# TensorE, VectorE and ScalarE in a written order beside the recurrent heads of a hybrid decoder layer

## The chip, the cores and the metric

One core of one Trainium2 chip runs the whole program. The metric is device time in microseconds; a comparison of two kernels takes the median over several runs. TensorE is called PE below, VectorE DVE, ScalarE ACT, GpSimd POOL; SP (SyncE) issues most of the DMA transfers, and "SPq" in the profile is its queue.

## The reference

One decoder layer over 1024 tokens, with 16 learned meta tokens ahead of them (L = 1040), model width 1024, feed-forward width 2816, all in float32:

```python
u = rmsnorm(h, mix_norm_pre)
q, f_logit, i_in, g_out, v_pool, gate_a, gate_b = split(u @ w_in)
a = hgrn2(q, f_logit, i_in, g_out, ...)       # 4 heads of width 128, gated linear recurrence
p = multiscale_pool(v_pool, pool_proj, scale) # 4 groups, trailing windows 2, 4, 8, 16
z = sigmoid(gate_a) * (a @ w_branch_hgrn) + sigmoid(gate_b) * (p @ w_branch_pool)
h = h + rmsnorm(z @ w_out, mix_norm_post)
u = rmsnorm(h, ffn_norm_pre)
gt = causal_dwconv(u @ ffn_w_gate)
h = h + rmsnorm((gelu(gt) * (u @ ffn_w_up)) @ ffn_w_down)
# hgrn2, each head: state = f_t * state + k_t v_t ; o_t = q_t state ; o * rsqrt(mean(o*o)) * gain * sigmoid(g)
```

## The kernel before

A float32 product is made of three PE passes on split operands: a tensor is split into a rounded part (`hi`, a copy on ACT) and the rest (`lo`, a subtraction on DVE), and hi·hi, lo·hi and hi·lo are summed in a bank of PSUM. So each block of weights is loaded raw (`wraw`), cast on ACT (`whi`) and subtracted on DVE (`wlo`) before PE can use it.

The stages by the profile's time: norm and the value projection (0 to 100 us), the projections for q, f and the two gates with a Strassen scheme (100 to 326), **the heads stage** (326 to 567), the mixer's output projection (567 to 690), the two Strassen products of the feed-forward (690 to 1100), and its down projection (1100 to the end).

The change is in the heads stage. `ORDER` is a string of steps that is walked in a loop:

- `PVn`, `Gn`, `PPn`, `BBn`, `BAn`: projections of the pooled values (`ppv`), of the output gates (`pg`), inside the pool groups (`ppp`), and the two branch products (`pbb`, `pba`). A letter p, q, r, s behind the kind is one quarter of one, a and b are halves.
- `hn`: the next step of head n (`head_steps`). The 64x64 scores of a chunk are built level by level: PE multiplies k and q (`level_mm`, tile `sl`), DVE grows k, q and f for the next level (`grow`), DVE or ACT takes the scores from PSUM (`level_out`, into `near` or `sc`). The first step issues the loads of f, q, kb and k, the next one multiplies q by f on DVE and then makes the first scores on PE (tile `sb`). After the levels come transposes (`pt`), state updates (`ds`, 7 chained operations on DVE), and the outputs (`po`): ACT takes `o` from PSUM, squares it into `rs` and casts that to `rh`; DVE subtracts to get `rl` and multiplies `o` by the gate. The last step sums the squares on PE (`ms`), takes Ln and Exp on ACT (`rs`), and DVE multiplies `o` by that.
- `spn`: pooling of a group on DVE and its split; `san`: split of a head's output into `ah`, `al`.
- `wn`: kept weights. While this stage runs, feed-forward weights of the first units are loaded, summed where the Strassen scheme wants it, split (ACT `whi`, DVE `wlo`) and stored to DRAM (`kept..h`, `kept..l`): `keep_first` for n under 4, `keep_unit` behind them.

Only PE is held to the order of this walk (`tc.manual_schedule(engines={E.PE})`); what ACT and DVE do is emitted by the same walk, but a scheduler sets the order on those two. SP issues loads in its own order, and each issue waits for the buffer that it fills. `Loader` keeps weights of up to three projections ahead, each loaded and split in one go.

`put_gate`, in the stage ahead, adds up a gate tile, takes its sigmoid on ACT and stores it to DRAM (`sscr`), issued from SP; a later `load_gate` reads it back.

Of the kernel before, what the change touches and what calls it, by code (L numbers as in the profile page):

```python
# [9 lines left out]
F32R = mybir.dt.float32r  # L10
U8 = mybir.dt.uint8
AF = mybir.ActivationFunctionType
# [40 lines left out]
ZA = 4  # L53
AHEAD = 3

ORDER = ("h0 h1 PV0 PVp1 PVq1 h0 PVr1 h1 PVs1 h0 PVp2 h1 PVq2 h0 sp0 PVr2 h1 PVs2 h0 PVp3 h1 sp1 PVq3 h0 PVr3 h1 "
# [4 lines left out]
POOLED = ()  # L61
VLOAD = 8
TRUNC = False
# [6 lines left out]
def trunk_kernel(ctx: ExitStack, tc: tile.TileContext, x, meta_tokens, mix_norm_pre,  # L70
# [25 lines left out]
    def nm(s):  # L96
        cnt[0] += 1
        return f"{s}_{cnt[0]}"
# [17 lines left out]
    def wraw_tile():  # L116
        return wst.tile([P, 1024], F32, tag="wraw", name=nm("wraw"), bufs=NRAW)
# [26 lines left out]
        return t  # L144


    def wsplit(src, n_k, n_c, eng=dve):
        raw = wst.tile([P, n_k * n_c], F32, tag="wraw", name=nm("wraw"), bufs=NRAW, padded_shape=[P, 1024])
        stage["load"] = nc.sync.dma_start(raw.rearrange("p (k c) -> p k c", k=n_k), src)
        hi = wst.tile([P, n_k * n_c], F32R, tag="whi", name=nm("whi"), padded_shape=[P, 1024])  # L150
        lo = wst.tile([P, n_k * n_c], F32R, tag="wlo", name=nm("wlo"), padded_shape=[P, 1024])
        act.copy(hi, raw)
        eng.tensor_tensor(lo, raw, rr(hi), ALU.subtract)
        return [(hi.rearrange("p (k c) -> p k c", k=n_k), lo.rearrange("p (k c) -> p k c", k=n_k))]

    def wsplit2(*srcs):

        raw, (hi, lo) = wraw_tile(), (wst.tile([P, 1024], F32R, tag=t, name=nm(t)) for t in ("whi", "wlo"))
        views = [[t[:, i * 512 : (i + 1) * 512].rearrange("p (k c) -> p k c", k=4) for t in (raw, hi, lo)] for i in range(2)]
        for (r, _, _), src in zip(views, srcs):  # L160
            stage["load"] = nc.sync.dma_start(r, src)
        act.copy(hi, raw)
        dve.tensor_tensor(lo, raw, rr(hi), ALU.subtract)
        return [(h, l) for _, h, l in views]

    class Loader:

# [5 lines left out]
        def ahead(self):  # L173
            while len(self.got) < min(len(self.srcs), self.at + AHEAD):
                self.got += self.get(*self.srcs[len(self.got)])

        def next(self):
            self.at += 1
            return self.got[self.at - 1]

    def wblock(w, k0, n_k, c0, n_c):
        return w[k0 * P : (k0 + n_k) * P, c0 : c0 + n_c].rearrange("(k p) c -> p k c", p=P)
# [427 lines left out]
    def eng(op):  # L610
        return pool_e if op in POOLED else dve
# [244 lines left out]
    def put_gate(u, i, h, a, b, c=None):  # L856
        kind, j = GUNITS[u]
        m, n = 2 * j + i, ghalo(u) + HN
        at = slice(n, n + HN) if h else slice(0, n)
        g = slot(at.stop - at.start, name="sg")  # L860
        dve.tensor_tensor(g, a, b, ALU.add)
        if c is not None:
            dve.tensor_tensor(g, g, c, ALU.add)
        if kind == "F":
            put_f(m, h, g)
            return
        if kind != "Q":
            act.activation(g, g, AF.Sigmoid)
        to = dict(Q=qdr, A=sd, B=sd)[kind]
        nc.sync.dma_start(to[m + (KD if kind == "B" else 0), :, at], g)  # L870

    def load_gate(d, b, m):
        d[m] = slot(TQ, name="sa")
# [17 lines left out]
    def job(kind, i):  # L891
        if kind == "G":
            return (wblock(WIN, 0, KD, CG + i * P, P), KD, u_q, CH_Q, lambda r: post_g(i, r))
        if kind == "PV":
            return (wblock(WIN, 0, KD, CV + i * P, P), KD, u_all, CH_ALL, lambda r: post_pv(i, r))
        if kind == "PP":
            return (pool_proj[0, i].rearrange("(k c) d -> c k d", k=1), 1,
                    lambda k, lo, n: (pin[i][0][:, lo : lo + n], pin[i][1][:, lo : lo + n]), CH_Q,
                    lambda r: post_pp(i, r))
        if kind == "BA":  # L900
            return (wblock(w_branch_hgrn[0], 0, HEADS, i * P, P), HEADS, a_x, CH_Q, lambda r: post_branch(sas, i, r))
        return (wblock(w_branch_pool[0], 0, HEADS, i * P, P), HEADS, p_x, CH_Q, lambda r: post_branch(sbs, i, r))
# [36 lines left out]
    def keep_first(u):  # L939
        raw = wst.tile([P, 1024], F32R, tag="wraw", name=nm("wraw"), bufs=NRAW)  # L940
        src = rr(raw).rearrange("p (k c) -> p k c", k=KD)
        nc.sync.dma_start(src, wblock(ffn_w_gate[0], 0, KD, 2 * u * P, P))
        keep(((u, "P1"), src[:, :4]), ((u, "P2"), src[:, 4:]), lo=raw)

    def keep_unit(u, w):
        ab = []
        for h in range(2):
            t = wraw_tile().rearrange("p (k c) -> p k c", k=4)
            nc.sync.dma_start(t, wblock(w, 4 * h, 4, 0, 2 * P))
            ab.append(t)  # L950
        a11, a21, a12, a22 = ab[0][:, :, :P], ab[0][:, :, P:], ab[1][:, :, :P], ab[1][:, :, P:]
        if u >= EARLY:
            keep(((u, "P1"), a11), ((u, "P2"), a12))
            yield
        ADD, SUB = ALU.add, ALU.subtract
        keep(((u, "P6"), ((a21, ADD, a22), (None, SUB, a11))), ((u, "P5"), ((a21, ADD, a22),)))
        yield
        keep(((u, "P3"), ((a21, ADD, a22), (None, SUB, a11), (a12, SUB, None))), ((u, "P7"), ((a11, SUB, a21),)))
        yield
        keep(((u, "P4"), a22))  # L960
        yield

    keeps = [keep_unit(0, ffn_w_gate[0]), keep_unit(UP0, ffn_w_up[0])]

    order = ORDER.split()
    order = [(o_[:-1], int(o_[-1])) for o_ in order]
# [59 lines left out]
    with tc.manual_schedule(engines={E.Activation, E.DVE, E.PE}):  # L1026
# [79 lines left out]
        for e in range(0, EARLY, 2):  # L1106
            p = gates.start_pair(e)
            for f in [f[i] for i in range(2) for f in p]:
                f()
                for j in SUMS_AT.get(13, ()) if e == 0 else ():  # L1110
# [5 lines left out]
    jobs_ = [(k.rstrip("ap"), i) for k, i in order if k[0].isupper() and k[-1] not in "bqrs"]  # L1116
    branch = [o_ for o_ in jobs_ if o_[0] in ("BA", "BB")]
    assert jobs_[-len(branch) :] == branch
    loader = Loader([job(*o_)[:2] + (P, eng("w%s%d" % o_)) for o_ in jobs_[: -len(branch)]]
                    + [tuple(job(*o_)[0] for o_ in branch[i - i % 2 : i - i % 2 + 2]) for i in range(len(branch))],  # L1120
                    lambda *a: wsplit(*a) if len(a) == 4 else wsplit2(*a))

    def split_z(c, k):
        n = len(TILES[c]) * P
# [11 lines left out]

    z0 = []
    gens, after, halves_of = {}, {}, {}
    with tc.manual_schedule(engines={E.PE}):
        for kind, i in order:  # L1140
            if kind == "sp":
                pool_split(i)
                continue
            if kind == "w":
                keep_first(i) if i < EARLY else next(keeps[i - EARLY])
                continue
            if kind == "sa":
                ahl[i] = split(heads[i]["o"], "a")
                continue
            if kind == "h":  # L1150
                if i not in gens:
                    gens[i] = head_steps(i)
                next(gens[i], None)
                continue
            kind, part = kind.rstrip("abpqrs"), kind[-1]
            src, n_k, xs, chunks, post = job(kind, i)
            if part in "qr":
                next(halves_of[kind, i])
                continue
            if part in "bs":  # L1160
                banks = next(halves_of[kind, i])
                loader.ahead()
                pay()
                after[kind, i] = post(banks)
                continue
            if kind in ("BA", "BB"):
                load_gate(sas if kind == "BA" else sbs, kind == "BB", i)
            ws = loader.next()
            if (kind, i) == ("BA", KD - 1):
                z0 = [split_z(0, k) for k in range(ZA)]  # L1170
            if part in "ap":
                halves_of[kind, i] = proj_parts(None, 0, n_k, xs, chunks, ws=ws, name="p" + kind.lower(),
                                                cuts=(n_k // 2,) if part == "a" else range(n_k // 4, n_k, n_k // 4))
                next(halves_of[kind, i])
                continue
            banks = proj(None, 0, n_k, xs, chunks, ws=ws, name="p" + kind.lower(),
                         by_bank=2 if (kind, i) == ("BA", KD - 1) else 0)
            loader.ahead()
            pay()
            after[kind, i] = post(banks)  # L1180
            if kind == "BA":
                dve.tensor_tensor(sas[i], sas[i], sbs[i], ALU.add)
                z[i] = sas[i]
# [622 lines left out]
```

## Time and profile before

| | us |
|---|---|
| median of 3 runs (lowest, highest) | 1319.91 (1318.8, 1320.88) |
| profiled execution, its own time | 1317.88 |
| span of the profiled execution | 1316.2 |
| PE busy | 1290.6 (98%) |
| DVE busy | 961.2 (73%) |
| ACT busy | 522.5 (40%) |
| POOL busy | 359.9 (27%) |

The time around the span is 1.7 us. PE is the engine with next to no idle time, so what another engine does costs only where PE waits for it. Durations of DVE and ACT instructions in the profile are those of one; queued behind each other they start about 0.09 us sooner than these add up to.

### The profile page before, as it was taken

To read this page: it belongs to the slowest core of one execution; us is meant where nothing else is said; L and a number is where in the kernel's file an instruction comes from. 1 tells how busy PE (TensorE), PEld (TensorE's weight loads), DVE (VectorE), ACT (ScalarE), POOL (GpSimd) and SP (SyncE) were. 2 spreads that over 40 slices of the span, in tenths; PEclk is the share of its full clock that TensorE was granted. 3 is DMA by queue.
4 is the path that set the end of the run, shared out by engine and by line. 5 is a ranking of instruction groups with operands and counts; after the bars stand their busy time and mean duration, and the time that the engine had idled before them with its cause. 6 is when DMAs were issued, how large, how long until landed. Compare 5 with 4: busy or idle time off the path is not lost.

```text
span 1316.2 us, 21988 instructions
## 1 busy us (share of the span) xinstructions
PE 1290.6 (98%) x8650; PEld 1139.7 (87%) x8650; DVE 961.2 (73%) x1293; ACT 522.5 (40%) x904; POOL 359.9 (27%) x307
## 2 busy tenths in 40 slices
PE   8999999999999899999999999999999999999998
PEld 7799899998998788978898888888888888888887
DVE  6768965454685887675588999888988985455758
ACT  5554533333134737226564222222332223444443
POOL 3015333230000000160035555554755652000000
PEclk9999999999999899999999999999999999999999
DMA  8135543334524566876677776667677699666644
GB/s 275 42 106 173 197 156 103 107 105 138 174 71 147 193 225 215 291 235 250 237 256 248 193 211 185 172 196 192 167 180 172 131 267 300 208 224 224 225 174 161
DMA packets 143802, 247.62 MB, mean 188 GB/s; under 512 B 11000, under 2 KB 75164, under 8 KB 143698
## 3 DMA queue, kind: packets, MB, share of 16 engines
q1 hardware_dynamic: 131634, 221.83, 49.6%
q0 software_dynamic: 12064, 24.38, 11.0%
q8 instruction: 68, 1.11, 0.3%
q14 instruction: 36, 0.29, 0.1%
HBM read 174.11 MB, written 95.09 MB: 205 GB/s over the span
## 4 chain that ended last, share of the span: by engine, by line
PE 91%; DVE 3%; DMA 2%; ACT 2%; issue 1%; SPq 0%; DVEq 0%; ACTq 0%
PE P L306 17%; PE P L307 17%; PE P L309 17%; PE pd L186 5%; PE pd L188 5%; PE pd L187 5%; PE pm L186 2%; PE pm L188 2%; PE pm L187 2%; PE ppv L206 1%; PE ppv L210 1%; PE pg L206 1%; PE ppv L207 1%; PE pv L187 1%; PE pv L186 1%
## 5 line engine op out<-in xcount | busy, mean ns | idle before, releaser
L307 PE MATMUL P<-v,whi 128*128 128x512 f32 (+2 forms) x408 | 140.7, 353 | 0.0
L306 PE MATMUL P<-v,whi 128*128 128x512 f32 (+2 forms) x408 | 140.7, 352 | 0.0
L309 PE MATMUL P<-v,wlo 128*128 128x512 f32 (+2 forms) x424 | 135.1, 349 | 0.0
L277 POOL TENSOR_TENSOR swa<-wraw,wraw 128x512 f32<-128x512 f32 x32 | 51.1, 1598 | 186.1 <-DMA wraw<-in_w_in_dram 79.8
L251 ACT CAST whi<-wraw 128x512 fp32r<-128x512 f32 x90 | 53.1, 618 | 102.4 <-PE P L307 75.9
L1516 DVE TENSOR_TENSOR rot<-wraw,rot 128x1024 fp32r<-128x1024 f32 x31 | 38.0, 1224 | 72.3 <-ACT rot L1515 72.3
L306 PEld LDWEIGHTS P<-v,whi 128*128 128x128 f32 x408 | 76.7, 188 | 10.4
L307 PEld LDWEIGHTS P<-v,whi 128*128 128x128 f32 x408 | 76.6, 188 | 10.2
L309 PEld LDWEIGHTS P<-v,wlo 128*128 128x128 f32 x424 | 74.0, 188 | 10.8
L187 PE MATMUL pd<-rot 128*128 128x512 f32 x274 | 82.5, 388 | 0.0
L188 PE MATMUL pd<-rot 128*128 128x512 f32 x274 | 82.5, 388 | 0.0
L186 PE MATMUL pd<-rot 128*128 128x512 f32 x274 | 81.9, 388 | 0.1
L252 DVE TENSOR_TENSOR wlo<-wraw,whi 128x512 fp32r<-128x512 f32 x86 | 76.4, 911 | 2.7 <-ACT whi L251 2.7
L251 ACT CAST whi<-swa 128x512 fp32r<-128x512 f32 x64 | 38.1, 619 | 92.6 <-PE P L307 77.8
L252 DVE TENSOR_TENSOR wlo<-swb,whi 128x512 fp32r<-128x512 f32 x64 | 66.4, 1045 | 10.4 <-ACT whi L251 10.4
L1515 ACT CAST rot<-wraw 128x1024 fp32r<-128x1024 f32 x31 | 32.7, 1054 | 90.8 <-PE pd L188 89.4
L306 PE MATMUL P<-uhi,whi 128*128 128x258 f32 (+2 forms) x240 | 68.5, 303 | 0.0
L307 PE MATMUL P<-ulo,whi 128*128 128x258 f32 (+2 forms) x240 | 68.4, 303 | 0.0
L251 ACT CAST whi<-swb 128x512 fp32r<-128x512 f32 x64 | 38.1, 618 | 71.6 <-PE P L307 67.1
L306 PE MATMUL P<-t4h,whi 128*128 128x258 f32 (+2 forms) x228 | 65.5, 304 | 0.0
L307 PE MATMUL P<-t4l,whi 128*128 128x258 f32 (+2 forms) x228 | 65.4, 304 | 0.0
L306 PE MATMUL P<-t2h,whi 128*128 128x258 f32 (+2 forms) x228 | 65.3, 304 | 0.0
(386 smaller groups left out, 3840.1 us busy)
## 6 DMA issues: line engine op xcount, KB each, us to landing
wraw<-in_w_in_dram SPq DMA_DIRECT2D x36, 512.0 KB, 4.2
yt<-ysum SPq DMA_DIRECT2D x33, 512.0 KB, 5.1
wraw<-in_ffn_w_gate_dram SPq DMA_DIRECT2D x26, 512.0 KB, 6.0
wraw<-in_ffn_w_up_dram SPq DMA_DIRECT2D x22, 512.0 KB, 6.0
wsum<-in_ffn_w_down_dram SPq DMA_DIRECT2D x22, 512.0 KB, 8.5
wraw<-in_w_out_dram SPq DMA_DIRECT2D x18, 512.0 KB, 4.4
ysum<-ys SPq DMA_DIRECT2D x11, 768.0 KB, 5.2
sa<-sscr SPq DMA_DIRECT2D x16, 513.0 KB, 5.3
```

Of the source, the lines that this page charges most:

```text
L186: pe.matmul(ps, ahi, bhi, start=first, stop=False)
L187: pe.matmul(ps, ahi, blo, start=False, stop=False)
L188: pe.matmul(ps, alo, bhi, start=False, stop=last)
L206: pe.matmul(ps[:, :n], whi[:, k, :], xhi, start=(k == 0), stop=False)
L251: act.copy(hi, src)
L252: (pool_e if 4 <= i < 2 * self.early else dve).tensor_tensor(lo, src, rr(hi), ALU.subtract)
L277: pool_e.tensor_tensor(s1, a21, a22, ALU.add)
L306: pe.matmul(d, whi[:, k, :], xh[:, c : c + w], start=(k == 0 and onto is None), stop=False, **go)
L307: pe.matmul(d, whi[:, k, :], xl[:, c : c + w], start=False, stop=False, **go)
L309: pe.matmul(x[:, o : o + w], wlo[:, k, :], xh[:, c : c + w], start=False, stop=(k == 3), **go)
L1515: act.copy(hi, src)
L1516: dve.tensor_tensor(lo, src, rr(hi), ALU.subtract)
```

## The change

It makes these edits:

- ACT and DVE join PE in the written order inside the heads stage: each takes its instructions in the order in which the walk emits them, and an instruction that waits holds up all that stands behind it on its engine.
- `ORDER` is written anew: heads 0 and 1 step every quarter from the start, heads 2 and 3 run on into the `BB` projections, the `BB` projections come as halves throughout, and the `w` steps are smaller and more.
- `Loader` becomes `Loader2`: the raw load is issued apart from the split, one projection further ahead; splits stay two ahead.
- `keep_first` and `keep_unit` yield between the load and the split.
- The sigmoid gates' stores are issued from ACT; the stores of `qdr` stay on SP.

```diff
-ORDER = ("h0 h1 PV0 PVp1 PVq1 h0 PVr1 h1 PVs1 h0 PVp2 h1 PVq2 h0 sp0 PVr2 h1 PVs2 h0 PVp3 h1 sp1 PVq3 h0 PVr3 h1 "
-         "PVs3 h0 sp2 Gp2 h1 Gq2 h0 h2 Gr2 h1 Gs2 h0 sp3 Gp3 h1 h2 Gq3 h0 h3 Gr3 h1 h2 Gs3 h0 PP0 h2 PP1 h1 h3 PP2 "
...
+ORDER = ("h0 h1 PVp0 PVq0 h0 PVr0 h1 PVs0 h0 PVp1 h1 PVq1 h0 PVr1 h1 PVs1 h0 sp0 PVp2 h1 PVq2 h0 sp1 PVr2 h1 PVs2 "
+         "h0 PVp3 h1 PVq3 h0 sp2 PVr3 h1 PVs3 h0 Gp2 h1 Gq2 h0 h2 sp3 Gr2 h1 Gs2 h0 h2 Gp3 h1 h3 Gq3 h0 h2 Gr3 h1 "
+         "h3 Gs3 h2 sa0 PP0 h3 PP1 h2 PP2 h3 sa1 PP3 h2 BBa0 h3 BBb0 h2 w0 BBa1 h3 BBb1 h2 w0 w1 BBa2 h3 BBb2 h2 w1 "
+         "w4 BBa3 h3 h2 w4 BBb3 h3 BBa4 h2 BBb4 h3 w4 BBa5 h2 BBb5 h3 w4 w5 BBa6 sa2 BBb6 h3 w5 BBa7 w5 BBb7 sa3 "
+         "BA0 w5 BA1 w5 w2 BA2 w2 w3 BA3 w3 BA4 BA5 BA6 BA7")
...
+    class Loader2:
+        def __init__(self, srcs):
+            self.srcs, self.raws, self.got, self.at, self.split = srcs, [], [], 0, 0
+            self.load()
+            self.load()
+            self.ahead()
...
+        def ahead(self):
+            while self.split < len(self.srcs) and len(self.got) < self.at + 2:
+                src, raw = self.srcs[self.split], self.raws[self.split]
+                self.got += wsplit2(raw) if len(src) == 2 else wsplit(*src[:3], raw=raw)
+                self.split += 1
+            if len(self.raws) <= self.split:
+                self.load()
...
-        if kind != "Q":
-            act.activation(g, g, AF.Sigmoid)
-        to = dict(Q=qdr, A=sd, B=sd)[kind]
-        nc.sync.dma_start(to[m + (KD if kind == "B" else 0), :, at], g)
+        if kind == "Q":
+            nc.sync.dma_start(qdr[m, :, at], g)
+            return
+        act.activation(g, g, AF.Sigmoid)
+        act.dma_start(sd[m + (KD if kind == "B" else 0), :, at], g)
...
         nc.sync.dma_start(src, wblock(ffn_w_gate[0], 0, KD, 2 * u * P, P))
+        yield
         keep(((u, "P1"), src[:, :4]), ((u, "P2"), src[:, 4:]), lo=raw)
+        yield
...
-    keeps = [keep_unit(0, ffn_w_gate[0]), keep_unit(UP0, ffn_w_up[0])]
+    keeps = [keep_first(u) for u in range(EARLY)] + [keep_unit(0, ffn_w_gate[0]), keep_unit(UP0, ffn_w_up[0])]
...
-    with tc.manual_schedule(engines={E.PE}):
+    with tc.manual_schedule(engines={E.PE, E.Activation, E.DVE}):
...
-                keep_first(i) if i < EARLY else next(keeps[i - EARLY])
+                next(keeps[i])
```

Line numbers in and behind the head steps grow by some 30 (L794, the gate product of `o`, becomes L825, L714 becomes L745, L802 becomes L833).

Two places are shown. The first is DVE around the outputs of head 0. In the kernel before, where `q_3400`, `k_3398` and `f_3397` are head 0, `..3408` head 1, `..4289` head 2, `..4500` head 3, and `o_4608` is head 0's output, it reads:

```order
L711 COPY_PREDICATED near_4417<-mask_145,sl_4543 128x64x2
L673 TENSOR_TENSOR k_4498<-k_4498,f_4497 128x528
L681 TENSOR_TENSOR f_4286<-f_4286 128x264
L771 SCALAR_TENSOR_TENSOR st_4523<-st_4523,f_3405,ds_4527 128x128
L153 TENSOR_TENSOR wlo_4601<-wraw_4598,whi_4600 128x128
L771 SCALAR_TENSOR_TENSOR st_4523<-st_4523,f_3405,ds_4536 128x128 x3
L153 TENSOR_TENSOR wlo_4656<-wraw_4653,whi_4655 128x128
L794 SCALAR_TENSOR_TENSOR o_4608<-o_4608,par,sg_4610 128x1026
L673 TENSOR_TENSOR k_4287<-k_4287,f_4286 128x132x4
L679 TENSOR_TENSOR q_4289<-q_4289,f_4286 128x128x4
L711 COPY_PREDICATED near_4417<-mask_152,sl_4666 128x32x4
```

Head 2 and head 3 were begun before head 0's output came: its product `o_4608` stands among level steps of head 2 and the state updates of head 1. In the changed kernel, where `o_4429` and `rl_4458` are head 0's, `q_4352` is head 2 and `o_4528`, `rl_4557` are head 1's, DVE reads:

```order
L157 TENSOR_TENSOR wlo_4420<-wraw_4247,whi_4419 128x128
L864 TENSOR_TENSOR rl_4458<-rs_4430,rh_4457 128x1026
L825 SCALAR_TENSOR_TENSOR o_4429<-o_4429,par,sg_4431 128x1026
L745 TENSOR_TENSOR q_4352<-q_4352,f_4349 128x512
L704 TENSOR_TENSOR k_4350<-k_4350,f_4349 128x528
L708 TENSOR_TENSOR q_4352<-q_4352,f_4349 128x1024
L712 TENSOR_TENSOR f_4349<-f_4349 128x528
L752 COPY_PREDICATED near_4465<-mbase,sb_4470 128x256
```

Now the first multiplication of head 2's q stands behind `rl` and the product of head 0. PE in the changed kernel has, at the same place, the outputs of head 0 (`po`), the first scores of head 2 (`sb`), and then the gate projection (`pg`):

```order
L820 MATMUL po_4446<-q_3396,st_4329 128x128
L819 MATMUL po_4446<-sc_3450,vh_3823 128x128
L820 MATMUL po_4446<-q_3396,st_4329 128x128
L750 MATMUL sb_4470<-q_4352,kb_4351 32x32 x32
L237 MATMUL pg_4507<-uhi_88,whi_4243 128x342
L238 MATMUL pg_4507<-ulo_89,whi_4243 128x342
```

No projection stands between `po` and `sb` there. The second place is DVE around the last step of heads 0 and 1. In the kernel before, head 3's first multiplication, of `q_4500`, stands among the state updates `st` of heads 0 and 1, with both outputs still to come:

```order
L681 TENSOR_TENSOR f_4286<-f_4286 128x528
L771 SCALAR_TENSOR_TENSOR st_4477<-st_4477,f_3397,ds_4481 128x128 x4
L771 SCALAR_TENSOR_TENSOR st_4477<-st_4477,f_3397,ds_4490 128x128 x3
L714 TENSOR_TENSOR q_4500<-q_4500,f_4497 128x512
L771 SCALAR_TENSOR_TENSOR st_4523<-st_4523,f_3405,ds_4527 128x128 x2
```

In the changed kernel the first multiplication of head 3 (`q_4564`) stands behind head 1's last product, `o_4528` by `rs_4529`:

```order
L712 TENSOR_TENSOR f_4349<-f_4349 128x264
L742 COPY_PREDICATED near_4465<-mask_145,sl_4601 128x64x2
L833 TENSOR_TENSOR o_4528<-o_4528,rs_4529 128x1026
L745 TENSOR_TENSOR q_4564<-q_4564,f_4561 128x512
L704 TENSOR_TENSOR k_4562<-k_4562,f_4561 128x528
L708 TENSOR_TENSOR q_4564<-q_4564,f_4561 128x1024
```

And PE there has the sums of squares of head 1 (`ms`), and directly behind them the first scores of head 3:

```order
L830 MATMUL ms_4660<-rl_4557,onesr 128x342
L829 MATMUL ms_4664<-rh_4556,onesr 128x342
L830 MATMUL ms_4664<-rl_4557,onesr 128x342
L750 MATMUL sb_4678<-q_4564,kb_4563 32x32 x32
L237 MATMUL pg_4507<-uhi_88,whi_4243 128x342
```

Head 3's scores moved from ahead of the outputs of heads 0 and 1 on DVE to behind the last operation of head 1.

More of the change, by code (lines that the diff above doesn't have):

```diff
@@ L144, in gain_bc, with wload, wsplit @@
         return t
-    def wsplit(src, n_k, n_c, eng=dve):
+    def wload(src, n_k, n_c):
         raw = wst.tile([P, n_k * n_c], F32, tag="wraw", name=nm("wraw"), bufs=NRAW, padded_shape=[P, 1024])
         stage["load"] = nc.sync.dma_start(raw.rearrange("p (k c) -> p k c", k=n_k), src)
+        return raw
+    def wsplit(src, n_k, n_c, eng=dve, raw=None):
+        raw = wload(src, n_k, n_c) if raw is None else raw
         hi = wst.tile([P, n_k * n_c], F32R, tag="whi", name=nm("whi"), padded_shape=[P, 1024])
@@ L154, in wsplit, with wload2, wsplit2 @@
         return [(hi.rearrange("p (k c) -> p k c", k=n_k), lo.rearrange("p (k c) -> p k c", k=n_k))]
[L156 to L161, printed above, removed]
+    def wload2(*srcs):
+        raw = wraw_tile()
+        for i, src in enumerate(srcs):
+            stage["load"] = nc.sync.dma_start(raw[:, i * 512 : (i + 1) * 512].rearrange("p (k c) -> p k c", k=4), src)
+        return raw
+    def wsplit2(raw):
+        hi, lo = (wst.tile([P, 1024], F32R, tag=t, name=nm(t)) for t in ("whi", "wlo"))
         act.copy(hi, raw)
         dve.tensor_tensor(lo, raw, rr(hi), ALU.subtract)
-        return [(h, l) for _, h, l in views]
+        return [tuple(t[:, i * 512 : (i + 1) * 512].rearrange("p (k c) -> p k c", k=4) for t in (hi, lo)) for i in range(2)]
     class Loader:
@@ L175, in ahead, with next, load @@
                 self.got += self.get(*self.srcs[len(self.got)])
+        def next(self):
+            self.at += 1
+            return self.got[self.at - 1]
+    class Loader2:
[4 more added lines that the diff above has]
+            self.ahead()
+        def load(self):
+            if len(self.raws) < len(self.srcs):
+                src = self.srcs[len(self.raws)]
+                self.raws.append(wload2(*src) if len(src) == 2 else wload(*src[:3]))
+        def ahead(self):
[5 more added lines that the diff above has]
+                self.load()
         def next(self):
@@ L950, in keep_unit @@
             ab.append(t)
+        yield
         a11, a21, a12, a22 = ab[0][:, :, :P], ab[0][:, :, P:], ab[1][:, :, :P], ab[1][:, :, P:]
@@ L1118, in trunk_kernel @@
     assert jobs_[-len(branch) :] == branch
-    loader = Loader([job(*o_)[:2] + (P, eng("w%s%d" % o_)) for o_ in jobs_[: -len(branch)]]
-                    + [tuple(job(*o_)[0] for o_ in branch[i - i % 2 : i - i % 2 + 2]) for i in range(len(branch))],
-                    lambda *a: wsplit(*a) if len(a) == 4 else wsplit2(*a))
+    loader = Loader2([job(*o_)[:2] + (P,) for o_ in jobs_[: -len(branch)]]
+                     + [tuple(job(*o_)[0] for o_ in branch[i - i % 2 : i - i % 2 + 2]) for i in range(0, len(branch), 2)])
     def split_z(c, k):
```

3 rows, old and new, of the table ORDER are left out of this document.

## The prediction

> **What bounds the kernel now.** I read the page first, its busy times and its chain of what ended last:
>
> ```profile
> span 1316.2 us, 21988 instructions
> PE 1290.6 (98%) x8650; PEld 1139.7 (87%) x8650; DVE 961.2 (73%) x1293; ACT 522.5 (40%) x904; POOL 359.9 (27%) x307
> PE 91%; DVE 3%; DMA 2%; ACT 2%; issue 1%; SPq 0%; DVEq 0%; ACTq 0%
> ```
>
> PE is idle for 25.6 us in all. The change takes no work from PE, so it can win only where PE waits or runs at a lower clock, and can lose wherever a new wait reaches PE. The next view is the table of busy times by stretch (us, then PE, PEld, DVE, ACT, POOL busy, the granted clock, DMA share, GB/s):
>
> ```profile
> 100.00:326.00 226.00, 225.32 (x1498) 207.98 (x1496) 144.73 (x193) 86.13 (x152) 71.06 (x49) 1.00 0.42 139
> 326.00:567.00 241.00, 227.34 (x2782) 216.57 (x2783) 173.44 (x291) 98.64 (x179) 11.44 (x22) 0.98 0.58 192
> ```
>
> The heads stage holds 241.00 − 227.34 = 13.66 us of idle PE; the gates stage ahead of it holds 0.68. DVE is busy 72% of the heads stage and ACT 41%, so neither is full; what matters is in which order they serve PE. The list of PE's waits between 320 and 567 us (total, times, longest) names the releasers:
>
> ```profile
> PE ms L798 <- DVE phis L842: 2.6, 1, 2.6
> PE po L788 <- DVE near L711: 2.0, 1, 2.0
> PE sl L696 <- ACT rs L800: 1.8, 1, 1.8
> PE sl L690 <- DVE q L679: 1.6, 1, 1.6
> PE sl L696 <- DVE near L711: 1.5, 1, 1.5
> PE pba L206 <- DVE sa L879: 1.2, 1, 1.2
> PE ms L799 <- DVE rl L833: 1.2, 1, 1.2
> ```
>
> All come from DVE or ACT; no row there names a weight (`whi`, `wlo`). The same table in finer stretches shows what a wait does to the clock:
>
> ```profile
> 425.90:426.70 0.80, 0.76 (x3) 0.79 (x4) 0.80 (x3) 0.80 (x3) 0.00 (x0) 0.50 0.50 200
> 426.70:429.20 2.50, 2.50 (x15) 2.50 (x14) 2.50 (x5) 0.03 (x1) 0.00 (x0) 0.53 0.02 7
> 441.00:443.00 2.00, 2.00 (x52) 1.96 (x45) 2.00 (x5) 1.97 (x3) 0.00 (x0) 0.50 0.70 264
> 443.00:446.00 3.00, 3.00 (x13) 3.00 (x12) 2.42 (x4) 2.73 (x4) 0.00 (x0) 0.50 0.31 110
> 450.00:470.00 20.00, 16.68 (x320) 15.18 (x319) 20.00 (x38) 10.79 (x18) 0.00 (x0) 1.00 0.65 212
> ```
>
> Behind the wait of 2.0 us (it ends at 425.9) PE runs at 0.50 to 0.53 for 3.3 us, which loses 0.8 × 0.5 + 2.5 × 0.47 = 1.6 us. Behind the two waits of 2.6 and 1.8 us the clock is 0.50 from 441 to 446, a loss of 2.5 us. Between 450 and 470, with 3.3 us idle in shorter pieces, it stays at 1.00. So the stage pays 13.7 + 1.6 + 2.5 = **17.8 us** for its waits. That is the ceiling of what the change can win here.
>
> **The change part by part.** First the edits that I cost at nothing. The gate stores leave SP for ACT:
>
> ```profile
> 324.60 0.32 SPq L870 DMA_DIRECT2D sscr<-sg  x1
> SPq L870 <- ACT sg L868: 43.1, 14, 6.7
> SPq L149 <- DVE wlo L153: 44.5, 6, 13.6
> ```
>
> One issue takes 0.32 us of SP; 32 of them are 10 us of ACT, in a stage of 226 us in which ACT has 140 us free. Even at twice the price (20 us) the cover holds, so nothing, between −0.7 (the stage's whole idle time) and +1. SP no longer stands behind sigmoids (43.1 us of waiting in the stretch from 250 us on), so loads behind these stores leave earlier; but no PE wait names a load. The same holds for the raw loads one projection ahead: SP waits 44.5 us there for a free buffer, and PE for none of those weights. Gain nothing; if the cover were gone it would show as PE waits for `wlo`.
>
> Now the written order. An instruction on DVE or ACT that waits now holds all that stands behind it. I walked the new order by hand from 326.2 us, with the durations of these rows:
>
> ```profile
> L833 DVE TENSOR_TENSOR rl<-rs,rh 128x1026 fp32r<-128x1026 f32 x4 | 4.9, 1218 | 0.0
> L794 DVE SCALAR_TENSOR_TENSOR o<-o,par,sg 128x1026 f32<-128x1026 f32 x4 | 5.1, 1285 | 1.8 <-ACT phis L841 1.3 <-ACT rs L792 0.5
> L802 DVE TENSOR_TENSOR o<-o,rs 128x1026 f32<-128x1026 f32 x4 | 4.9, 1225 | 2.4 <-ACT rs L801 2.4
> L714 DVE TENSOR_TENSOR q<-q,f 128x512 f32<-128x512 f32 x4 | 2.8, 688 | 6.0 <-DMA q<-qscr 6.0
> L819 DVE TENSOR_TENSOR_SCAN s<-vp 128x1040 f32<-128x1040 f32 x3 | 6.9, 2309 | 0.0
> L801 ACT ACTIVATE rs<-rs 128x1026 f32<-128x1026 f32 x4 | 4.2, 1062 | 0.0
> ```
>
> *First place, outputs of head 0.* PE goes from `po` of head 0 straight to `sb` of head 2, which needs `q`; on DVE that stands behind head 0's `rl` and `o`. ACT's timeline shows the chain ahead of `rl` in the kernel before, for head 1:
>
> ```profile
> 431.26 0.59 ACT L791 COPY o<-po 128x512 f32<-128x512 f32 x1 [1.20 <-PE po L789]
> 431.88 1.06 ACT L792 ACTIVATE rs<-o 128x1026 f32<-128x1026 f32 x1
> 432.97 1.06 ACT L832 CAST rh<-rs 128x1026 fp32r<-128x1026 f32 x1
> ```
>
> From the last `po` the copy, the square and the cast take 432.97 + 1.06 − 431.26 = 2.8 us, then DVE 1.22 + 1.29 + 0.69 = 3.2: 6.0 us, less 0.2 for overlapped starts, in which PE has nothing: **5.8 us** (6.4 if nothing overlaps and each hand-over costs 0.1).
>
> *Second place, last step of head 1.* PE goes from `ms` straight to `sb` of head 3. Its `q` stands on DVE behind head 1's last product, and that waits for Ln, a table load and Exp on ACT:
>
> ```profile
> 439.95 1.42 ACT L800 ACTIVATE rs<-ms,eps_t 128x342 f32<-128x342 f32 x3
> 441.39 1.28 ACT L801 ACT_TABLE_LOAD   x1
> ```
>
> The last of three Ln (1.42 / 3 = 0.5), the load 1.28, Exp 1.06, then DVE 1.23 + 0.69: 4.8 us from the last `ms`. If the first table load (the Ln side, as long) isn't done ahead, all three Ln come late: 4.8 + 0.9 + 1.28, 7.0. I take **5.3**, nearer to the lower end, since the first load waits for no data. [...]
>
> Both places leave PE idle for longer than any wait of before, so the clock must fall behind each: 1.6 to 2.5 us each by the rows above, 2.1 taken, **4.2** for both. [...]
>
> *Start of the stage.* The order has `sb` of head 1 after three quarters only. DVE's timeline of before:
>
> ```profile
> 335.04 0.71 DVE L673 TENSOR_TENSOR k<-k,f 128x528 f32<-128x528 f32 x1 [2.85 <-DMA k<-kscr]
> 337.70 0.69 DVE L714 TENSOR_TENSOR q<-q,f 128x512 f32<-128x512 f32 x1 [1.94 <-DMA q<-qscr]
> ```
>
> These DVE waits are for DMA; PE stood on other projections. In the new order PE reaches `sb` of head 1 at about 335.5, an estimate of three quarters and a first `sb` behind 326.2; `q` of head 1 lies on DVE behind head 0's k and three more operations. With the loads 1.6 us earlier (no sigmoid ahead of them on SP), it is ready at 337 to 338: **2.0 us**, between 0 and 3.5, and clock 0.8 (0 to 1.6).
>
> *Around 380 us.* The level steps of head 0 stand on DVE behind a `wlo` (1.23) that waits for ACT, and a pooling scan (2.31): 3.5 us of foreign work less what a PE quarter covers. **2.0**, 0 to 3.5.
>
> *PP projections, and the rest up to the BB ones.* The nearest rows are the waits at L798 and L696 (2.6 and 1.8) in the same part. **2.0**, 0 to 4.
>
> *Kept weights.* `w` steps put `wlo` and `whi` of feed-forward weights on DVE and ACT between the additions that free PE's banks (`sa`, L879). They wait for loads that SP issues behind stores of other kept weights:
>
> ```profile
> SPq L937 <- ACT whi L922: 35.6, 12, 5.1
> L920 DVE TENSOR_TENSOR wlo<-wraw,wraw 128x512 f32<-128x512 f32 x6 | 4.0, 687 | 6.1 <-DMA wraw<-in_ffn_w_gate_dram 3.6 <-DMA kept7l<-wlo 2.5
> ```
>
> Before, DVE could do another addition meanwhile; PE waited 1.2 us for L879. Now a late load delays all of them. At worst two of SP's longest waits or so (5.1 + 3.6, about 8); at best nothing, since loads are issued a step ahead. **3.0.**
>
> Sum of what is new: 5.8 + 5.3 + 4.2 + 2.0 + 0.8 + 2.0 + 2.0 + 3.0 = 25.1 us. I count all of the 17.8 as gone, since each of those waits came of where the scheduler had put a DVE or ACT operation. The balance is +7.3: 1317.88 + 7.3 = 1325.2 for a profiled execution, whose own time lies 2.0 under the median of the runs shown, so **1327** against the median.
>
> **The rivals.** *Faster: PE waits at the two places only.* If loads are early enough and every other new wait is covered by the projection beside it, and the clock doesn't fall, the new cost is 5.8 + 5.3 = 11.1 against 17.8: 1319.9 − 6.7 = 1313. For it speaks that DVE has 28% of the stage free and that heads 0 and 1 start earlier; against it the clock rows, and the DMA waits on DVE at the start. *No change.* The two places with their clock (15.3) and 2.0 in the PP part, nothing else: 17.3 against 17.8, 1319. *Kept weights decide.* If SP's stores delay the loads by its longest waits, that term is 8 and the clock falls again (2.5), 7.5 more than forecast: 1335; it decides once the loads land over 3 us behind the addition that follows. For it speaks a DMA share of 0.58 over the stage, against it the loads issued a step ahead. That the change might do less than it says is only possible for the stores and loads, which I count at nothing anyway.
>
> **How the numbers follow.** Forecast 1327: 0.48. Faster rival 1313: 0.30. No change 1319: 0.10. Kept weights 1335: 0.12. A change of 0.2% (2.6 us) is about what the measurement tells from none: faster 0.30, same 0.10, slower 0.60. The range: below the forecast it takes in the faster rival with one of its two places 4 us shorter, 1309; above, the start, 380, PP and table-load terms at their upper ends with the kept weights at theirs would give 1327 + 2.3 + 1.5 + 2 + 1.7 + 7.5 = 1342, and as they won't all meet I end at 1338. The forecast's own case spans 1321 to 1333.
>
> **What would show it.** Right: PE idle for 5 to 6 us between the `po` of head 0 and the next `sb`, released by DVE `q`, with a granted clock near 0.5 behind it; the same behind `ms` of head 1; the waits at L711 and L842 gone. ACT in the gates stage longer busy, PE there unchanged. Wrong: PE idle in the stage under 10 us in all, or `q` of heads 2 and 3 done before these places; or waits of PE for `whi`, `wlo`, which I count at nothing.

## The result, and the profile after

The changed kernel is slower: 1.0279 of the time before (95% interval 1.0242 to 1.0316), 1352 to 1361 us against 1320.4 in the same comparison. One execution of it at 2143 us and a clock of 0.556 is left out of the ratio. The profiled execution took 1352.1 us, 34.2 more than that of before. The direction was as forecast, the size was not: 7 us were forecast.

The page of the changed kernel, its busy times and its chain that ended last:

```profile
span 1350.4 us, 21954 instructions
PE 1299.5 (96%) x8650; PEld 1147.6 (85%) x8650; DVE 969.1 (72%) x1293; ACT 524.4 (39%) x905; POOL 353.3 (26%) x307
PE 64%; DVE 3%; ACT 3%; issue 1%; DMA 1%; DVEq 0%; SPq 0%; ACTq 0%
```

PE's idle time went from 25.6 to 50.9 us, and the same 8650 matmul records now take 8.9 us longer: 25.3 + 8.9 is the whole difference. Nearly all of both lies in the heads stage, which now ends at about 601 us (table of busy times by stretch):

```profile
335.00:343.00 8.00, 7.92 (x159) 7.59 (x160) 4.77 (x7) 0.00 (x0) 0.34 (x4) 0.80 0.59 228
420.00:430.00 10.00, 9.96 (x122) 9.71 (x123) 2.84 (x4) 1.36 (x4) 0.00 (x0) 0.82 0.01 2
440.00:450.00 10.00, 5.70 (x147) 5.43 (x147) 5.63 (x9) 4.72 (x7) 0.00 (x0) 0.66 0.09 26
500.00:510.00 10.00, 3.62 (x13) 3.62 (x14) 4.63 (x8) 2.34 (x5) 0.00 (x0) 0.50 0.51 196
326.00:601.00 275.00, 235.64 (x2792) 224.37 (x2792) 177.42 (x293) 101.06 (x181) 9.02 (x21) 0.93 0.48 162
100.00:326.00 226.00, 225.62 (x1499) 208.09 (x1498) 145.76 (x193) 85.88 (x152) 70.10 (x49) 1.00 0.43 138
```

275.00 − 235.64 is 39.4 us idle, against 13.7 before, at a mean clock of 0.93. The gates stage ahead, with the stores now on ACT, is as it was. PE's waits in the changed kernel (total, times, longest):

```profile
PE sb L750 <- issue: 12.6, 2, 6.6
PE pbb L237 <- ACT kt L783: 10.4, 1, 10.4
PE po L819 <- ACT rs L831: 3.0, 1, 3.0
PE sl L721 <- DVE q L710: 2.8, 1, 2.8
PE pm L217 <- DVE sa L911: 2.3, 1, 2.3
PE sb L750 <- DMA kb<-kbscr: 2.3, 1, 2.3
...
PE pba L238 <- DVE al L864: 1.8, 1, 1.8
...
PE pba L237 <- ACT ah L863: 1.1, 1, 1.1
```

The two `sb` waits are the two places of the forecast. "issue" means that the view names no releaser; the timelines of ACT and then DVE do. At the first place:

```profile
414.12 0.59 ACT L822 COPY o<-po 128x512 f32<-128x512 f32 x1 [1.20 <-PE po L820]
414.74 1.06 ACT L823 ACTIVATE rs<-o 128x1026 f32<-128x1026 f32 x1
415.83 1.05 ACT L863 CAST rh<-rs 128x1026 fp32r<-128x1026 f32 x1
```

```profile
416.91 1.23 DVE L864 TENSOR_TENSOR rl<-rs,rh 128x1026 fp32r<-128x1026 f32 x1 [6.01 <-ACT rh L863]
418.05 1.28 DVE L825 SCALAR_TENSOR_TENSOR o<-o,par,sg 128x1026 f32<-128x1026 f32 x1
419.25 0.69 DVE L745 TENSOR_TENSOR q<-q,f 128x512 f32<-128x512 f32 x1
```

DVE stands idle for 6.0 us, with head 2's `q` ready to be done (its load was issued at 393.99, and the slowest of the four such loads landed after 6.4 us), because head 0's `rl` is first in line; PE starts `sb` at 420.04, 5.96 us after its last `po`.

The 10.4 us lie at 496 to 506. The chain of waits there, in order of time:

```profile
488.54 9.24 DMA kept1l<-wraw
497.86 3.87 DMA wraw<-in_ffn_w_gate_dram
501.76 0.70 DVE wlo L952
...
505.84 0.49 ACT kt L783
506.38 0.65 PE pbb L237
```

And SP's own wait:

```profile
SPq L983 <- DMA kept1l<-wraw: 7.9, 1, 7.9
```

A store of kept weights holds one of the three raw buffers; the second load of the next unit (`w4`) can be issued only when that store has landed, 9.2 us after its issue. DVE waits 8.1 us in line with the sum `wlo` for that load, ACT 13.1 us in line with the cast behind it, and behind them stand the operations that free PE's banks: `sa` on DVE and `kt` on ACT. PE, out of banks, waits its 10.4 us for `kt`.

### The profile page after: what moved, and what is told of

It is laid out like the page before. It is cut to its first block, busy times and chain, and to the rows that moved or that the text cites. A ratio compares the mean times of both kernels' runs of the same rounds, so it can differ in the third digit from the quotient of the medians.

```text
span 1350.4 us, 21954 instructions
## 1 busy us (share of the span) xinstructions
PE 1299.5 (96%) x8650; PEld 1147.6 (85%) x8650; DVE 969.1 (72%) x1293; ACT 524.4 (39%) x905; POOL 353.3 (26%) x307
## 4 chain that ended last, share of the span: by engine, by line
PE 64%; DVE 3%; ACT 3%; issue 1%; DMA 1%; DVEq 0%; SPq 0%; ACTq 0%
PE P L338 11%; PE P L337 11%; PE P L340 11%; PE pd L217 5%; PE pd L219 5%; PE pd L218 5%; PE pm L217 2%; PE pm L219 2%; PE pm L218 2%; PE pba L238 1%; PE pba L237 1%; PE pba L241 1%; PE pbb L237 1%; PE pbb L241 1%; DMA kept1l<-wraw 1%
## 5 line engine op out<-in xcount | busy, mean ns | idle before, releaser
L337 PEld LDWEIGHTS P<-v,whi 128*128 128x128 f32 x408 | 76.7, 188 | 10.4
```

The source lines that it names most:

```text
L337: pe.matmul(d, whi[:, k, :], xh[:, c : c + w], start=(k == 0 and onto is None), stop=False, **go)
```

## The experiments

**DVE and ACT to the scheduler, all else as changed.**

```diff
-    with tc.manual_schedule(engines={E.PE, E.Activation, E.DVE}):
+    with tc.manual_schedule(engines={E.PE}):
```

> The changed kernel, but DVE and ACT are left to the scheduler again in the heads stage; the new ORDER, the loads ahead, the kept weights in pieces and the stores from ACT stay. Theory A (the written order on DVE and ACT makes the stalls, since an instruction that waits holds all behind it): the waits of 6.0 us before sb of head 2 and 6.6 us before sb of head 3 and the wait of 10.4 us at pbb shrink to below 3 us each, and the time falls from about 1356 to 1315-1328 us. Theory B (the new ORDER, the loads or the stores are what costs, whoever orders DVE): the waits stay and the time stays above 1345 us.

Measured: 1314.8 us, ratio to before 0.9961 (0.9948 to 0.9974). Theory A holds: the written order on these two engines costs 3.2% (1.0279 / 0.9961 = 1.032), about 42 us, and what is left of the change wins 0.4%. PE's largest waits there:

```profile
PE sb L750 <- DMA kb<-kbscr: 2.8, 2, 1.6
PE sb L750 <- ACT rs L831: 2.0, 1, 2.0
PE ms L830 <- DVE rl L864: 1.5, 1, 1.5
```

**One engine at a time.** `engines={E.PE, E.Activation}`:

> The changed kernel with ACT and PE in the written order and DVE left to the scheduler. Theory A says that the cost is DVE's line (q of heads 2 and 3 behind products of heads 0 and 1): most of the 42 us between the changed kernel (1356) and the version with both left to the scheduler (1315) goes, 1317 to 1332 us. If ACT's line is what costs (its casts of kept weights ahead of evictions), it stays above 1340.

`engines={E.PE, E.DVE}`:

> The changed kernel with DVE and PE in the written order and ACT left to the scheduler. Theory A: the waits before sb of heads 2 and 3 (6.0 and 6.6 us) stay nearly whole, since DVE still waits in line for Square, Ln and Exp, and so does the wait behind the kept weights' load: 1340 to 1358 us. If ACT's line is what costs: below 1332.

Measured: 1328.6 us with ACT in line (1.0060, 1.0045 to 1.0076), 1339.6 with DVE in line (1.0138, 1.0112 to 1.0163). Against both free (0.9961) that is 1.0% and 1.8%, some 13 and 23 us of the 42. With DVE alone in line the `sb` waits are whole, the one behind the load at `pbb` is gone, and a new one stands behind the sums of the kept weights, for head 3's `al`:

```profile
PE sb L750 <- issue: 12.6, 2, 6.6
PE pba L238 <- DVE al L864: 5.8, 1, 5.8
```

With ACT alone in line 2.0 us are left of the `sb` waits, as with both engines free, and of the 10.4 us 3.6 are left, at a later `po`, since `kt` still stands on ACT behind a cast that waits for a sum of the kept weights:

```profile
PE po L819 <- ACT kt L783: 3.6, 1, 3.6
```

The two `sb` waits are DVE's line. The 10.4 us come only with both in line; each line alone has a smaller wait behind the kept weights. The two parts add up to 36 of the 42 us, and both hold a longer wait at the mixer's start (`pm`, 5.8 us with DVE in line and 4.2 with ACT, against 0.7). The lists name DVE's `sa` as what released PE there. DVE's part lay a little under the expected stretch, since I had expected that wait to stay too.

**Heads 2 and 3 moved ahead.**

```diff
-Gs2 h0 h2 Gp3 ... Gr3 h1 h3 Gs3
+Gs2 h2 h0 Gp3 ... Gr3 h3 h1 Gs3
```

> The changed kernel with head 2's step moved ahead of head 0's outputs, and head 3's ahead of head 1's last step, in ORDER; all else as changed. Theory A says that the two waits of 6.0 and 6.6 us and the lower clock behind them (about 3.5 us more) go: 14 to 16 us less than the changed kernel, about 1341 us. Rival: the chain from po over ACT to DVE only meets the next PE instruction that needs DVE, and less than 6 us are won, above 1350 us.

Measured: 1350.4 us (1.0235, 1.0208 to 1.0261), about 6 us won, the rival's side of the forecast, though hardly clear of the noise (the interval overlaps that of the changed kernel). DVE's timeline shows why the second place is only half mended, 4.6 us in place of 6.6:

```profile
434.19 1.23 DVE L833 TENSOR_TENSOR o<-o,rs 128x1026 f32<-128x1026 f32 x1 [2.68 <-ACT rs L832]
...
437.46 0.71 DVE L745 TENSOR_TENSOR q<-q,f 128x512 f32<-128x512 f32 x1
```

Head 3's `q` now stands behind head 0's last product, which waits for Exp as head 1's did. And PE's wait at the mixer's start (`pm`) grew from 2.3 to 7.3 us. There the timelines of DVE and POOL show splits of z that take 0.41 us elsewhere:

```profile
589.33 2.64 DVE L1163 TENSOR_TENSOR zc<-sa,zc 128x256 fp32r<-128x256 f32 x1
...
592.37 5.38 DVE L1163 TENSOR_TENSOR zc<-sa,zc 128x256 fp32r<-128x256 f32 x1
```

```profile
588.28 3.40 POOL L1258 TENSOR_TENSOR wlo<-wraw,whi 128x1024 fp32r<-128x1024 f32 x1 [153.29 <-ACT whi L1256]
...
592.78 4.67 POOL L1258 TENSOR_TENSOR wlo<-wraw,whi 128x1024 fp32r<-128x1024 f32 x2
```

**The same, with that subtraction on DVE.**

```diff
-            pool_e.tensor_tensor(lo, raw, rr(hi), ALU.subtract)
+            dve.tensor_tensor(lo, raw, rr(hi), ALU.subtract)
```

> The version with heads 2 and 3 moved ahead, and the low part of the first output weights (w_out) subtracted on DVE in place of GpSimd. In the version without this, DVE's small splits of z took 2.64 and 5.38 us in place of 0.41 while GpSimd subtracted, and PE waited 7.3 us for them. If the two engines stand in each other's way there: the splits take 0.41 us, PE's wait at pm falls below 3 us, and the time is 1343 to 1347 us against 1350.4. If the splits are long for another reason: the wait stays and the time is 1350 or more.

Measured: 1344.0 us (1.0180, 1.0164 to 1.0197), 6.4 less; no split of z is over 0.56 us, and `pm` waits 2.4:

```profile
L1163 DVE TENSOR_TENSOR zc<-sa,zc x24: 417/549/561, 588.1 to 674.0; 128x384 fp32r<-128x384 f32 x16, 128x256 fp32r<-128x256 f32 x8
PE pm L217 <- DVE sa L911: 2.4, 1, 2.4
```

By these runs about half of what the move of the heads had won was lost at the end of the stage, where DVE met GpSimd; the eight subtractions of output weights on DVE, 1.22 us in each of the three that its timeline up to 600 us shows, cost less. Both edits together win 12 us, near theory A's 14 to 16. The changed kernel with the second edit alone was not run, so how much of the 6.4 us would come there too stays open.

**One sum of the kept weights later.**

```diff
-BBa3 h3 h2 w4 BBb3 h3 BBa4 h2 BBb4 h3 w4 BBa5
+BBa3 h3 h2 BBb3 h3 BBa4 h2 BBb4 h3 w4 w4 BBa5
```

> The changed kernel with one step of the kept weights, the split of the first unit's sums that waited for its load (w4, second step), moved 2 projections later, beside the next w4 step. Theory C (the 10.4 us wait is DVE and ACT standing in line behind a load that SP could issue only when a store of another kept weight had freed the buffer): the wait of 10.4 us goes, and 8 to 13 us are won with its clock, about 1346 us. Rival: the load is later still by its neighbours on the DMA queues and the wait only moves to the new place: over 1352 us.

Measured: 1347.7 us (1.0210, 1.0180 to 1.0241), 9 less, within theory C's stretch. The 10.4 us are gone, but another wait grew from 3.0 to 7.7:

```profile
PE po L819 <- ACT rs L831: 7.7, 1, 7.7
```

Here Ln of head 2 stands on ACT behind casts of the kept weights, and these behind the sums on DVE. So the load was the cause of the long wait, and the sums themselves, in line, are the next one.

**All named places mended, all three engines in line.**

```diff
-Gs2 h0 h2 Gp3 h1 h3 Gq3 h0 h2 Gr3 h1 h3 Gs3 h2 sa0 PP0 h3 PP1 h2 PP2 h3 sa1 PP3
+h2 Gs2 h0 Gp3 h1 h3 Gq3 h2 Gr3 h3 h0 h1 Gs3 h2 PP0 h3 PP1 sa0 h2 PP2 h3 PP3 sa1
...
(w4 from its second step on, and w5, w2 and w3, some projections later)
```

> All three engines in the written order as in the changed kernel, with the named places mended in ORDER: head 2's first scores a projection quarter ahead of head 0's outputs, head 3's ahead of the last steps of both heads 0 and 1, the splits of heads 0 and 1 two projections later, and the sums of the kept weights behind the last of the heads' steps. If the named waits are the cause (theories A and C), of the 12.6 us before sb some 10 go, of the 10.4 and 3.0 us behind the kept weights some 12, and of the lower clock some 5: 1326 to 1334 us. Rival: a written order only hands a wait on to the next instruction that needs DVE, as in the two runs that mended one place each (6 and 9 us won): 1338 to 1348 us.

Measured: 1347.5 us (1.0211, 1.0195 to 1.0226): the rival. One of the `sb` waits is still 4.2 us, and most of the others are new ones; all PE waits of the stage add up to 32.4 us, against 39.8 in the changed kernel. The longest:

```profile
PE sb L750 <- DVE q L745: 5.8, 2, 4.2
PE pbb L237 <- ACT rs L831: 5.8, 1, 5.8
PE pba L237 <- ACT whi L168: 3.9, 2, 3.4
PE sb L750 <- DMA kb<-kbscr: 3.9, 2, 2.5
PE pba L237 <- DVE sa L911: 3.6, 3, 2.0
PE ppp L237 <- ACT sg L655: 3.0, 1, 3.0
```

That two lines cannot be written well by hand is not shown by this; it is shown that none of these four versions, mended at their longest waits, comes near the scheduler.

**The small edits.** The gate stores from ACT, alone on the kernel before (the `put_gate` part of the diff):

> The kernel before, with nothing but the gate stores issued from ACT. All theories: within 0.2% of before, 1317 to 1323 us, since no wait of PE names a load in the heads stage. If the 32 issues on ACT delay the weights' casts in the gates stage, PE would wait for whi there and the time would rise by over 3 us.

Measured: 1319.5 us, ratio 1.0003 (0.9992 to 1.0014). Nothing, as forecast. `Loader2` alone on the kernel before:

> The kernel before with the changed kernel's loader alone (raw loads a projection ahead, splits two ahead). If the 4.9 us by which the loader tells the two versions with the new ORDER apart is its own: 1313 to 1317 us. If it is worth nothing by itself, as forecast, and only meets the new ORDER well: 1318 to 1322 us.

Measured: 1319.5, ratio 0.9995 (0.9984 to 1.0005). Nothing either. The loader of before with the new ORDER, DVE and ACT to the scheduler:

> DVE and ACT left to the scheduler, the new ORDER, but the loader of the kernel before (load and split in one go, three projections ahead). If the raw loads one projection ahead are worth nothing, as forecast: 1313.5 to 1316.5 us, as the version with the new loader (1314.8). If the 4.4 us won over the kernel before come of the loader: back at 1318 to 1320.

Measured: 0.9994 (0.9979 to 1.0008). So the new ORDER alone wins nothing and the new loader alone wins nothing; only together do they win the 0.4%. In the profile the mixer's start (`pm`) waits 3.6 us with the old loader and 0.7 with the new one. Why the two need each other stays open, the more so as the runs with the old loader spread over 9 us.

**Versions beyond.** Heads 2 and 3 ahead, DVE and ACT to the scheduler:

> The new ORDER with head 2's step ahead of head 0's outputs and head 3's ahead of head 1's last step, DVE and ACT left to the scheduler. If PE's remaining wait of 2.0 us before sb of head 3 there goes with nothing in its place: 1311 to 1314 us, against 1314.8 without the move. Rival: the scheduler places head 3's q early anyway and its po waits instead: 1314 to 1317.

Measured: 1315.8 us, 0.9963 (0.9949 to 0.9978): the same as without it. The wait before `sb` is now 3.0 us, not gone. Heads 0 and 1 a quarter later:

```diff
-PVp0 PVq0 h0 PVr0 h1 PVs0 h0 PVp1 ... h1 h3 Gs3 h2
+PVp0 PVq0 PVr0 h0 PVs0 h1 PVp1 h0 ... h0 h3 Gs3 h1 h2
```

> The new ORDER with DVE and ACT left to the scheduler, and all steps of heads 0 and 1 one projection quarter later, up to the PP projections. In the version without the shift PE waits 2.8 us for kb at the first scores and 2.0 us before sb of head 3. If both go: 1309.5 to 1312 us. If the heads' end comes later by the quarter and is missed at the end of the BB projections: 1314 to 1318 us.

Measured: 1314.2 us, 0.9956 (0.9941 to 0.9971). Both leading `sb` waits shrink (1.6 us in all), `ppp` waits longer; it is the fastest one here and beats both kernels, though not clearly the version with nothing shifted.

## Why the prediction was wrong

**What held.** That written lines on DVE and ACT turn their waits into PE's was right at the two places and at 380 us, where a `wlo` that waits for ACT and then a scan stand on DVE ahead of a head's level steps, as forecast. Term by term, in us of idle PE: first place 5.8 forecast, 6.0 measured; second 5.3, 6.6; at 380 us 2.0, 2.8; PP projections and the rest 2.0, 2.6 (four waits of 0.4 to 1.0, for which no instruction had been named). The stores were worth nothing, as the row of the gates stage and the run with them alone show. The waits of before are gone, as forecast, but for 0.9 us at the first `ppv`.

The start agrees by luck, 2.0 and 2.3. The forecast had head 1's scores late, behind three quarters; they came without a wait. PE waited before the scores of head 0, which `ORDER` puts behind two quarters, for a load:

```profile
335.04 1.08 PE L750 MATMUL sb<-q,kb 128*32 128x32 f32 x64 [2.26 <-DMA kb<-kbscr]
```

The kernel before has no such wait, and with DVE and ACT left to the scheduler it stays (2.8 us, in the list of that run): it comes of the new `ORDER`, not of the written lines.

On ACT the second place reads:

```profile
437.25 1.28 ACT L831 ACT_TABLE_LOAD   x1
438.55 1.42 ACT L831 ACTIVATE rs<-ms,eps_t 128x342 f32<-128x342 f32 x3
439.98 1.28 ACT L832 ACT_TABLE_LOAD   x1
441.27 1.06 ACT L832 ACTIVATE rs<-rs 128x1026 f32<-128x1026 f32 x1
```

That is the chain of the forecast, and longer than its 5.3 because ACT came to head 1's Ln only after head 0's Ln and Exp, each with a table load of its own, so that the load for its Ln was not done ahead. The forecast had this case, at 7.0, and took a value near its lower end. Each load took 1.28 us, and the one of the Exp began 0.01 us behind the Ln. That a load can stand done ahead of its data the kernel before shows: there one ran from 499.58 to 500.86 us, and its Ln, waiting for `ms`, began at 502.29.

**What failed: the term for the kept weights.** It was 3.0, with 8 at most. Measured: 10.4 + 3.0 + 1.1 + 1.8 = 16.3 us, in all of which PE stood behind kept-weight work in the two lines: for `kt` and `sa`, for head 2's Ln, and for head 3's `ah` and `al`. ACT's timeline at the second of these waits:

```profile
529.88 0.62 ACT L954 CAST whi<-wlo 128x512 fp32r<-128x512 f32 x1 [1.36 <-DVE wlo L952]
530.51 1.28 ACT L831 ACT_TABLE_LOAD   x1
```

The mechanism was named, with its end (banks freed late; for `ah` and `al` it was operands that came late); what I mis-sized was the load. I took it as issued a step ahead and priced its delay by SP's longest waits of before (5.1 + 3.6). In the kernel before such a wait is covered, since the scheduler gives DVE something else; so its rows hold no such price. The new one is 9.2 us for the store, then 3.9 for the load, then the sums, one behind the other. It was priced as one late load; PE waited in four places.

**And the clock.** The forecast had 5.0 us for it (4.2 and 0.8), in place of 4.1 that went. PE's busy time grew by 8.9, so the clock took about 13 in all, an estimate that takes the 4.1 as gone: after the 10.4 us it stood at 0.50 for the rest of 500 to 510, and after the start it cost 1.6 (8 us at 0.80) where 0.8 was taken. Behind the 3.0 us and behind the 1.1 and 1.8 it was 0.83 (530 to 540 and 550 to 560). So most of the missed waits cost twice, but not each of them: behind the 2.8 us at 384 us the clock stayed at 1.00.

**What was not in it.** 2.3 us at the mixer's start, for which no term stood. A DVE split of z that takes 0.15 us elsewhere took 2.37 there, while GpSimd subtracted (from 596.86 us, for 2.71):

```profile
597.22 2.37 DVE L1167 TENSOR_TENSOR zc<-sa,zc 128x2 fp32r<-128x2 f32 x1
```

No run takes this out of the changed kernel by itself, so its price there is read from the trace alone.

Sum: 38.9 us of idle PE are in these terms, against 20.1 forecast. With the 0.9 us at `ppv` it is 39.8; 0.4 of that lie behind 601 us, and the rest are the stage's 39.4. The kept-weights case was among the rivals, at 1335 and a chance of 0.12, and its price had the same fault.

## What to carry to other kernels

To put an engine in written order is to let every wait of it hold all that stands behind (here PE stood 6.0 and 6.6 us for it at the two places); before doing it, look in the profile at what that engine waits for, not at what PE waits for, since the waits that are now covered by other work are the price, and they stand in no list of PE's waits. Work for a later stage (loads, sums and stores of weights) should not stand in one line with operations that free the banks of the busiest engine: the 10.4 us here came of that. And price a chain through DMA by its links, store landing, buffer, load landing (here 9.2 and 3.9 us), rather than by the longest wait seen so far.

## What the runs showed of the hardware

DVE's splits of z and GpSimd's subtractions took longer where they overlapped. With heads 2 and 3 moved ahead, a DVE subtraction of 128x256 that takes 0.41 us took 2.64 and 5.38 us while GpSimd subtracted 128x1024 (the 5.38 us overlap two of these), and it took 0.42 with that subtraction moved to DVE. GpSimd's own subtraction took 3.40 us beside the 2.64; the median of the eight in the changed kernel is 2.40. Why, the traces do not show.

The lower clock did not follow a wait's length alone: after 2.0 us in the kernel before it was 0.50, while after 2.8 us in the changed one it stayed at 1.00 (the wait ends at 384.12):

```profile
380.00:385.00 5.00, 2.20 (x24) 1.95 (x23) 4.96 (x7) 1.66 (x5) 0.00 (x0) 1.00 0.05 13
385.00:400.00 15.00, 15.00 (x111) 14.37 (x109) 9.16 (x12) 6.59 (x13) 0.10 (x1) 1.00 0.38 128
```
